# Gates of all dense tiles but one added into cleared DRAM by indirect DMAs, and 65 of 256 candidate sums

## Chip, cores and metric

The kernel runs on one core of a Trainium2 chip. The metric is the device time of one execution in microseconds (us). Names of engines: PE is TensorE, DVE is VectorE, ACT is ScalarE, POOL is GpSimd, SP is SyncE, which here only issues DMAs. ACT and POOL issue DMAs too.

## What is computed

Two layers of a trunk over 256 context tokens and 512 latent tokens, 1024 features wide: a mixer (attention and a short convolution in layer 0, an mLSTM in layer 1), and after each a feed-forward block that selects experts (PEER). The change lies in the PEER blocks:

```python
q = (xb @ w_q).reshape(PEER_BLOCK, PEER_HEADS, 2, PEER_DHALF)      # 8 heads, 2 halves
s = jnp.einsum('thpd,hpkd->thpk', q, subkeys)                      # 128 scores per half
s1, i1 = lax.top_k(s[:, :, 0], PEER_TOPK)                          # 16 of 128
s2, i2 = lax.top_k(s[:, :, 1], PEER_TOPK)
cand = (s1[..., :, None] + s2[..., None, :]).reshape(..., 256)     # 16 x 16 sums
cidx = (i1[..., :, None] * 128 + i2[..., None, :]).reshape(..., 256)
top, pos = lax.top_k(cand, PEER_TOPK)                              # 16 of 256
idx = jnp.take_along_axis(cidx, pos, axis=-1)
g = jax.nn.softmax(top, axis=-1)
act = jax.nn.gelu(jnp.einsum('td,thkd->thk', xb, u[idx]), approximate=False)
return jnp.einsum('thk,thkd->td', g * act, v[idx])
```

So each token takes 8 x 16 of 16,384 experts.

## The kernel before

**Tiles.** 128 tokens are one tile; the block of layer 0 has six tiles, that of layer 1 has four. Of these, `NG` = 2 and 1 are gathered: for each of the 128 (head, k) columns of a tile one indirect DMA on POOL's queue fetches 128 rows of `u` (512 KB, tile `urows`, `dot`, L899), and DVE multiplies them with the tokens (L905). The other tiles, four and three, are dense: all 16,384 rows of `u` and `v` pass PE.

**Two stages of a block.** `peer_u` runs over 128 chunks of 128 experts. In chunk c, SP loads `uf`, ACT and DVE split it into `uh` and `ul`, PE multiplies the dense tokens with it (24 matmuls, `proj`, L674), and ACT writes the Gelu to DRAM (`gad`). Chunks 0 to 16 also hold the 16 projection steps: `w_q` and `subk` are loaded and split (`q_load`, the low parts on POOL), PE projects all tokens, and DVE finds the 16 best of 128 scores for each tile (`topk16`). `peer_v0` and `peer_v1` then run over 128 chunks of `v`: they load `gad` and the gates `gd`, multiply them on DVE and feed PE.

**Gates.** A dense tile needs its gates as a matrix over tokens and experts. `stage2` finds the 16 best of 256 sums (`cands`, `decode`, `soft`). Then DVE writes one-hot matrices for eight tokens at a time (`prep`, L834 to L837, four instructions), PE multiplies them (`gbuild`, L851: 256 small matmuls for a tile), ACT copies the product into `stg`, and ACT's queue stores it into `gd`, 512 KB at a time.

**What sets the order.** `peer_u` shares out the work of routing, gates and gathered dots over the chunks: each item has a cost, each chunk has a budget (`slack`), and the queue with the largest share left goes next. `issue_after` ties an item to the split of the next chunk. A scheduler then fixes the sequence of each engine. Each engine runs its own sequence strictly in order. A DMA issued by SP or ACT counts on one of eight semaphores, which are taken in turn, and one issued by POOL on one of eight others; before a semaphore is used again, the DMA that used it last must have landed.

Of the kernel before, what the change touches and what calls it, by code (L numbers as in the profile page):

```python
# [10 lines left out]
F32 = mybir.dt.float32  # L11
# [10 lines left out]
P = 128  # L22
# [40 lines left out]
NG = (2, 1)  # L63
SEGS = ((0, NCTX), (NCTX, NLAT))
# [7 lines left out]
def kernel(ctx: ExitStack, tc: tile.TileContext, a: dict, out: bass.AP, dbg=None, stop=None):  # L72
# [13 lines left out]
    tok = [a["tok"][t * P:(t + 1) * P, :] for t in range(NT)]  # L86

# [125 lines left out]
    def mixer0(pk_open):  # L213
        with ExitStack() as st:
            rst = ExitStack()
            mcp = mkpool(st, "m0mc")
            mch = mcp.tile([P, 4, T], F32R, name="mch")
            mcl = mcp.tile([P, 4, T], F32R, name="mcl")
# [10 lines left out]
            with ExitStack() as s1:  # L229
# [225 lines left out]
            with ExitStack() as st2:  # L455
# [193 lines left out]
    def peer_u(layer, tiles):  # L649
# [4 lines left out]
        gd = dram.tile([TD // 32, P, P, 32], F32, name=f"gd{layer}")  # L654
# [3 lines left out]
        with ExitStack() as s1:  # L658
# [9 lines left out]
            def proj(ps, wh, wl, blks):  # L668
                for k in range(KD):
                    for x, q in ((wh, 0), (wh, 1), (wl, 0)):  # L670
# [9 lines left out]
                      allow_small_or_imprecise_dtypes=True)  # L680
            urow = [up.tile([P, P], U32, name=f"urow{j}", bufs=1) for j in range(ng)]
            gact = [up.tile([P, P], F32, name=f"gact{j}", bufs=1) for j in range(ng)]
# [5 lines left out]
            def q_load(hp):  # L688
# [4 lines left out]
                split(wh, wl, w, eng_lo=vec if hp < 2 else pool)  # L693
# [4 lines left out]
                split(skh, skl, sk, eng_lo=pool)  # L698
# [42 lines left out]
            side, pend, stores = [], [], []  # L741

            def store():
                b, stg, j = stores.pop(0)
                js = slice(j, j + P // GS)
                nc.scalar.dma_start(gd[b][:, js], stg[:, js])
# [5 lines left out]
            def stage2(t):  # L752
                d = {}

                def alloc():
                    d["top"] = up.tile([P, PH, TOPK], F32, name="top", bufs=3)
                    d["pos"] = up.tile([P, PH, TOPK], U32, name="pos", bufs=3)
                    d["if"] = up.tile([P, 16, TOPK], F16, name="if16", bufs=3)
                    d["id"] = [up.tile([P, PH, TOPK], F32, name=f"id{q}", bufs=3) for q in range(2)]

                def cands(h0):
                    def f():
                        vv = v16[t].rearrange("p (h q) k -> p h q k", q=2)
                        c = up.tile([P, 2, TOPK, TOPK], F32, name="cand", bufs=1)
                        hs = slice(h0, h0 + 2)
                        vec.tensor_tensor(c, vv[:, hs, 0, :, None].to_broadcast([P, 2, TOPK, TOPK]),
                                          vv[:, hs, 1, None, :].to_broadcast([P, 2, TOPK, TOPK]), op=ALU.add)
                        for h in range(2):
                            w_ = up.tile([P, 256], F32, name="candw", bufs=1)
                            topk16(d["top"][:, h0 + h, :], d["pos"][:, h0 + h, :],  # L770
                                   c[:, h].rearrange("p x y -> p (x y)"), w_)
                    return f

                def decode(h0):
                    def f():
                        iv = d["if"].rearrange("p (h q) k -> p h q k", q=2)
                        hs = slice(h0, h0 + 2)
                        qs = slice(2 * h0, 2 * h0 + 4)
                        vec.tensor_copy(d["if"][:, qs], i16[t][:, qs])
                        for q in range(2):  # L780
                            pi = up.tile([P, 2, TOPK], U32, name="pi")
                            if q == 0:
# [855 lines left out]
```

## Time and profile before

| | before |
|---|---|
| median of 3 runs | 4072.93 us (4070.59 to 4076.04) |
| profiled execution | 4070.86 us, of which the span of its instructions is 4069.1 us |
| `peer_u`, layer 0: projection steps | 475 to 785 us |
| `peer_u`, layer 0: the other 111 chunks | 785 to 1604 us |
| `peer_v0` | 1632 to 2310 us |
| `peer_u`, layer 1: the other 111 chunks | 2942 to 3504 us |
| `peer_v1` | 3549 to 4045 us |

Each stage has its own limit, so the shares of the whole span say little; the stages are read apart. A row with an arrow in brackets gives the idle time of an engine just before an instruction and what ended it. The chain of waits is followed back from the last instruction and shows, at each time, the work that nothing else would have hidden.

### The profile page before, as it was taken

What the parts mean: (1) busy time and instruction counts of PE and PEld (TensorE: products, weight loads), DVE (VectorE), ACT (ScalarE), POOL (GpSimd) and SP (SyncE); (2) the same over time, 40 slices, a digit from 0 to 9 for tenths busy, and PEclk for the clock granted to TensorE, in tenths of its full rate; (3) what the DMA queues carried; (4) which work ended last, traced back from release to release, by engine and by line L of the source; (5) the groups of instructions that cost most, each with busy time, mean ns of one, the idle gap of its engine ahead of it and who ended that gap; (6) DMA issues with size and microseconds to landing.
All of it is one profiled execution on the core that took longest, in us unless ns stands there. A gap on an engine that the chain in (4) does not pass through costs nothing. (4 is left out here: it accounts for less than half of the span.)

```text
span 4069.1 us, 53545 instructions
## 1 busy us (share of the span) xinstructions
PE 3779.4 (93%) x19201; PEld 3221.3 (79%) x19201; DVE 3287.3 (81%) x6594; ACT 1463.4 (36%) x2384; POOL 1394.4 (34%) x1010
## 2 busy tenths in 40 slices
PE   6988989999999897999999989888999999899998
PEld 5766777877777675788888789867899999788887
DVE  7776698998999897888888864458898987588887
ACT  4354422233232333322232355542234344333333
POOL 2521225303423244666666412215302222132221
PEclk9999989999999998999999999988999999999999
DMA  7301446548979799999999721046448779799995
GB/s 245 100 3 52 172 141 240 177 167 301 342 261 356 274 368 363 387 390 390 387 391 389 283 84 46 18 172 220 164 159 319 266 268 331 286 385 363 356 356 216
DMA packets 409099, 1036.47 MB, mean 255 GB/s; under 512 B 33024, under 2 KB 167680, under 8 KB 408832
## 3 DMA queue, kind: packets, MB, share of 16 engines
q1 hardware_dynamic: 259360, 498.68, 35.3%
q0 software_dynamic: 114336, 416.34, 27.9%
q10 hardware_dynamic: 35136, 118.05, 7.5%
q8 instruction: 150, 2.46, 0.2%
q14 instruction: 117, 0.96, 0.1%
HBM read 906.05 MB, written 126.88 MB: 254 GB/s over the span
## 5 line engine op out<-in xcount | busy, mean ns | idle before, releaser
L899 POOL DMA_INDIRECT urows<-in_u_rows,urow x384 | 487.5, 1270 | 1124.1 <-DVE urows L905 639.4
L1048 POOL DMA_INDIRECT vrows<-in_v_t,vrow x384 | 594.2, 1547 | 592.5 <-DVE accg L1056 340.1
L674 PE MATMUL aps<-pnh,uh 128*128 128x512 f32 (+1 forms) x2048 | 770.0, 376 | 22.0 <-ACT ga L991 18.4
L674 PE MATMUL aps<-pnh,ul 128*128 128x512 f32 (+1 forms) x2048 | 763.6, 373 | 26.3 <-DVE ul L109 26.0
L674 PE MATMUL aps<-pnl,uh 128*128 128x512 f32 (+1 forms) x2048 | 759.6, 371 | 0.0
L106 ACT CAST uh<-uf 128x1024 fp32r<-128x1024 f32 x256 | 269.2, 1051 | 839.2 <-PE aps L674 815.9
L905 DVE SCALAR_TENSOR_TENSOR urows<-urows,px 128x1024 f32<-128x1024 f32 x384 | 468.7, 1231 | 66.1 <-DMA urows<-in_u_rows,urow 65.4
L106 ACT CAST vh<-vf 128x1024 fp32r<-128x1024 f32 x256 | 269.3, 1053 | 594.5 <-DMA vf<-in_v_t 279.9
L674 PEld LDWEIGHTS aps<-pnh,ul 128*128 128x128 f32 x2048 | 389.8, 190 | 78.7 <-DVE ul L109 34.2
L674 PEld LDWEIGHTS aps<-pnh,uh 128*128 128x128 f32 x2048 | 391.5, 191 | 72.0 <-ACT ga L991 25.4
L109 DVE TENSOR_TENSOR vl<-vf,vh 128x1024 fp32r<-128x1024 f32 x256 | 312.6, 1221 | 166.0 <-ACT vh L106 155.9
L674 PEld LDWEIGHTS aps<-pnl,uh 128*128 128x128 f32 x2048 | 390.5, 191 | 43.2
L109 DVE TENSOR_TENSOR ul<-uf,uh 128x1024 fp32r<-128x1024 f32 x256 | 320.2, 1251 | 79.5 <-ACT uh L106 70.3
L1079 PE MATMUL acc<-vh,vwh 128*128 128x512 f32 x1024 | 317.7, 392 | 23.9 <-ACT vwh L106 23.8
L1079 PE MATMUL acc<-vh,vwl 128*128 128x512 f32 x1024 | 317.3, 391 | 1.3 <-DVE vwl L109 1.1
L1079 PE MATMUL acc<-vl,vwh 128*128 128x512 f32 x1024 | 317.5, 391 | 0.0
L1056 DVE SCALAR_TENSOR_TENSOR vacc<-vrows,gw,vacc 128x1024 f32<-128x1024 f32 x254 | 313.8, 1277 | 0.0
L851 PE MATMUL gps<-p,p 128*128 128x128 f16 x1792 | 243.9, 296 | 14.1 <-DVE p L837 14.1
L1144 PE MATMUL acc<-vh,vwh 128*128 128x512 f32 x768 | 239.3, 393 | 15.2 <-ACT vwh L106 12.1
L1079 PEld LDWEIGHTS acc<-vh,vwh 128*128 128x128 f32 x1024 | 192.8, 189 | 66.2 <-ACT vwh L106 26.4
L851 PEld LDWEIGHTS <-p 128*128 128x128 f16 x1792 | 189.1, 118 | 62.7 <-issue 38.6
L1144 PE MATMUL acc<-vl,vwh 128*128 128x512 f32 x768 | 238.2, 392 | 0.0
(430 smaller groups left out, 7540.8 us busy)
## 6 DMA issues: line engine op xcount, KB each, us to landing
uf<-in_u_t SPq DMA_DIRECT2D x256, 512.0 KB
vf<-in_v_t SPq DMA_DIRECT2D x256, 512.0 KB
gd<-stg ACTq DMA_DIRECT2D x112, 512.0 KB
wmt<-in_w_modT SPq DMA_DIRECT2D x90, 512.0 KB
gad<-ga ACTq DMA_DIRECT2D x64, 512.0 KB
gaf<-gad SPq DMA_DIRECT2D x64, 512.0 KB
gf<-gd SPq DMA_DIRECT2D x32, 1024.0 KB
gad<-ga ACTq DMA_DIRECT2D x64, 384.0 KB
```

Of the source, the lines that this page charges most:

```text
L106: act.copy(hi, src)
L109: return el.tensor_tensor(lo, src, hi.bitcast(F32), op=ALU.subtract)
L674: pe.matmul(ps[:, o:o + w], x[:, k, :], blk[q][:, k, :w], start=(k == 0 and x is wh and q == 0), stop=(k == KD - 1 and x is wl))
L851: pe.matmul(gp[:, i * P:(i + 1) * P], p1[:, g, :, i], p2[q][:, g, :, i], start=q == 0, stop=q == 1)
L899: nc.gpsimd.indirect_dma_start(out=r, out_offset=None, in_=a["u_rows"], in_offset=bass.IndirectOffsetOnAxis(ap=urow[j][:, k:k + 1], axis=0))
L905: vec.scalar_tensor_tensor(r, r, 1.0, PK["x"][j], op0=ALU.mult, op1=ALU.mult, accum_out=gact[j][:, k:k + 1])
L1048: nc.gpsimd.indirect_dma_start(out=r, out_offset=None, in_=a["v_t"].rearrange("l c k d -> (l c k) d"), in_offset=bass.IndirectOffsetOnAxis ...
L1056: vec.scalar_tensor_tensor(acc, r, gw[:, k:k + 1], acc, op0=ALU.mult, op1=ALU.add)
L1079: pe.matmul(acc[i][hf], x[:, ts_], y[:, hf * 512:(hf + 1) * 512], start=(c == 0 and first), stop=(c == 127 and end))
L1144: pe.matmul(acc[i][hf], x[:, ts_], y[:, hf * 512:(hf + 1) * 512], start=(c == 0 and first), stop=(c == 127 and last))
```

## The change

`NOH` = 1 dense tile keeps the one-hot products. For the others (three in layer 0, two in layer 1) five DRAM tiles of 4 x 128 x 128 x 32 floats, 8.4 MB each, are first set to zero by `clear`, a DMA on ACT's queue. When half of a tile's heads are routed, `spots` (DVE) computes for each token and (head, k) the place of its gate. `scatter` then issues an indirect DMA on POOL's queue for one (head, k): it adds 128 floats, one of each token, to their places. A tile has 128 such DMAs, so there are 384 in layer 0 and 256 in layer 1. Two of them on the same tile may hit the same place, and the later one waits until the earlier has landed; `scatter` goes round the tiles that are ready. A quota spreads them over the chunks up to `SC_END` = 122.

Candidate sums: only pairs whose ranks can be among the best 16 are formed, 65 of 256, for two or four heads at a time. `q_load` splits on DVE instead of POOL. In a projection step `topk16` comes last. The shares are now four queues with a chunk to begin and one to end each (`goal`), and the next item is that of the queue which lags most, in us.

```diff
+NOH = 1
+SC_END = 122
...
+    gds = [[dram.tile([4, P, P, 32], F32, name=f"gd{v}_{t}") for t in range(n - NG[v])]
+           for v, n in enumerate((NT, NLAT // P))]
+
+    def clear(v, t, zero):
+        nc.scalar.dma_start(gds[v][t].rearrange("b p j t -> (b p j t)").rearrange("(p x t) -> p x t", p=P, t=P),
+                            zero[:, None, :].to_broadcast([P, P, P]))
...
                 for j in range(3):
                     conv(j)
+                    if NOH + j < len(gds[0]):
+                        clear(0, NOH + j, zero)
...
+                    if h < len(gds[1]) - NOH:
+                        clear(1, NOH + h, zero)
...
-                split(wh, wl, w, eng_lo=vec if hp < 2 else pool)
+                split(wh, wl, w)
...
+                        c = up.tile([P, H, 65], F32, name="cand", bufs=1)
+                        for o, r0, rn, m in ((0, 0, 1, 16), (16, 1, 2, 8), (32, 3, 4, 4), (48, 7, 8, 2), (64, 15, 1, 1)):
+                            vec.tensor_tensor(c[:, :, o:o + rn * m].rearrange("p h (r m) -> p h r m", m=m),
...
+                def spots(h0):
+                    def f():
+                        ks, (i0, i1) = ids(h0)
+                        rf = up.tile([P, 4 * TOPK], F32, name="rowf", bufs=1)
+                        vec.tensor_scalar(rf, i0, float(P * 32), spos[:, 0:1], op0=ALU.mult, op1=ALU.add)
+                        vec.scalar_tensor_tensor(srow[t][:, ks], i1, 32.0, rf, op0=ALU.mult, op1=ALU.add)
+                        ready[t] += range(ks.start, ks.stop)
+                    return f
...
+                    return [(cands(h0), 1.6 * H, need), (decode(h0), 0.7 + 1.4 * H, need), (soft(h0), 1.0, need)] + \
+                        ([(last, 0.5, need)] if last else [])
...
+            queues = [route, one, dots, bgq]
+            goal = [(4, 66), (17, 114), (6, 125), (17, 124)]
...
+            def lag(q, c):
+                c0, c1 = goal[q]
+                want = min(max((reach[c] - reach[c0]) / (reach[c1] - reach[c0]), 0.0), 1.0)
+                return want * whole[q] - (whole[q] - left[q])
...
+                nc.gpsimd.indirect_dma_start(
+                    out=gd[t - ng].rearrange("b p j (t o) -> (b p j t) o", o=1),
+                    out_offset=bass.IndirectOffsetOnAxis(ap=srow[t][:, k:k + 1], axis=0),
+                    in_=g[:, k:k + 1], in_offset=None, compute_op=ALU.add)
...
+                quota = (scat - sent["n"]) if c == 127 else -(-(scat - sent["n"]) // max(SC_END - c, 1))
...
-                    q = max(ok, key=lambda q: left[q] / whole[q])
+                    q = max(ok, key=lambda q: lag(q, c))
...
+                    if quota > 0 and w > 1.0 and scatter():
+                        quota -= 1
+                while quota > 0 and scatter():
+                    quota -= 1
...
-            nc.sync.dma_start(st["gf"], gd[:, :, c:c + 4, :].rearrange("b p j t -> p b j t"))
+            for t, x in enumerate(gd):
+                nc.sync.dma_start(st["gf"][:, 4 * t:4 * t + 4], x[:, :, c:c + 4, :].rearrange("b p j t -> p b j t"))
```

The sequence of the engines shows where the new DMAs stand. A row is a line of the kernel, an operation and its tiles (with buffer numbers), and the semaphores that it waits for.

POOL in the middle of `peer_u`, layer 0. Before, gathers alone:

```order
L899 DMA urows_9351<-in_u_rows,urow1_4266 128x1024 [waits DMASW1_49,DVE_49]
L899 DMA urows_9354<-in_u_rows,urow0_4265 128x1024 [waits DMASW2_49,DVE_49]
L899 DMA urows_9390<-in_u_rows,urow1_4266 128x1024 [waits DMASW3_49,DVE_49]
L899 DMA urows_9401<-in_u_rows,urow0_4265 128x1024 [waits DMASW4_49,DVE_49]
L899 DMA urows_9442<-in_u_rows,urow1_4266 128x1024 [waits DMASW5_49,DVE_49]
```

In the change (`gd0_1` to `gd0_3` are the three tiles that take the sums, `srow` the places):

```order
L944 DMA urows_8641<-in_u_rows,urow1_4297 128x1024 [waits DMASW3_49,DVE_49]
L1030 DMA gd0_1_79<-g3_4304,srow3_4298 2097152x1 [waits DMASW0_49]
L1030 DMA gd0_3_81<-g5_4306,srow5_4300 2097152x1 [waits DMASW1_49]
L1030 DMA gd0_2_80<-g4_4305,srow4_4299 2097152x1 [waits DMASW2_49]
L944 DMA urows_8680<-in_u_rows,urow0_4296 128x1024 [waits DMASW7_49,DVE_49]
L1030 DMA gd0_1_79<-g3_4304,srow3_4298 2097152x1 [waits DMASW4_49]
```

Three scatters now stand between two gathers, and each waits for the scatter on its own tile four places ahead of it.

POOL at the end of `peer_u`, layer 0. Before, the last gathers of `u` are followed by loads and gathers of `peer_v0`:

```order
L899 DMA urows_13932<-in_u_rows,urow0_4265 128x1024 [waits DMASW6_49,DVE_49]
L899 DMA urows_13935<-in_u_rows,urow1_4266 128x1024 [waits DMASW7_49,DVE_49]
L1085 DMA vht_19664<-hd0_0_60 128x1024 [waits DMASW0_49,PE_49]
L1085 DMA vht_19679<-hd0_1_61 128x1024 [waits DMASW1_49]
L1048 DMA vrows_14370<-in_v_t,vrow0_3506 128x1024 [waits DMASW2_49,Pool_49]
```

In the change:

```order
L944 DMA urows_13114<-in_u_rows,urow0_4296 128x1024 [waits DMASW6_49,DVE_49]
L1030 DMA gd0_3_81<-g5_4306,srow5_4300 2097152x1 [waits DMASW7_49,DVE_49]
L944 DMA urows_13120<-in_u_rows,urow1_4297 128x1024 [waits DMASW0_49,DVE_49]
L1030 DMA gd0_3_81<-g5_4306,srow5_4300 2097152x1 [waits DMASW7_49,DMASW1_49]
L1030 DMA gd0_3_81<-g5_4306,srow5_4300 2097152x1 [waits DMASW2_49,DMASW1_49]
L1169 DMA vht_18783<-hd0_0_60 128x1024 [waits DMASW3_49,PE_49]
L1030 DMA gd0_3_81<-g5_4306,srow5_4300 2097152x1 [waits DMASW4_49,DMASW2_49]
```

64 scatters on one tile stand here in a row, behind all gathers of the stage but one; each waits for the one before it.

SP at the start of the program. Before:

```order
L272 DMA xn2_164<-in_tok 128x1024 [waits DMAHW1_49]
L148 DMA wmt_168<-in_w_modT 128x1024 [waits DMAHW2_49]
L253 DMA wmp_175<-in_w_mod0 128x1024 [waits DMAHW3_49]
L272 DMA xn3_186<-in_tok 128x1024 [waits DMAHW4_49]
L272 DMA xn4_190<-in_tok 128x1024 [waits DMAHW5_49]
```

In the change, where ACT's third DMA is the first clear (`gd0_1`), which counts on DMAHW4:

```order
L282 DMA xn2_173<-in_tok 128x1024 [waits DMAHW2_49]
L156 DMA wmt_177<-in_w_modT 128x1024 [waits DMAHW3_49]
L263 DMA wmp_184<-in_w_mod0 128x1024 [waits DMAHW4_49]
L282 DMA xn3_195<-in_tok 128x1024 [waits DMAHW5_49]
L282 DMA xn4_199<-in_tok 128x1024 [waits DMAHW6_49]
```

The load of `wmp` now waits for the clear, and the loads behind it wait with it.

## Rows read from the trace of the kernel before

**Rows 1.** The page: each engine's busy time, share and instructions
```profile
PE 3779.4 (93%) x19201; PEld 3221.3 (79%) x19201; DVE 3287.3 (81%) x6594; ACT 1463.4 (36%) x2384; POOL 1394.4 (34%) x1010
```

**Rows 2.** Busy time by stage; the first row names the columns
```profile
core 0: us, PE busy (x) PEld busy (x) DVE busy (x) ACT busy (x) POOL busy (x), PEclk, DMA share, GB/s
475.00:785.00 310.00, 283.46 (x1463) 243.48 (x1464) 272.99 (x995) 76.24 (x117) 124.63 (x89) 0.93 0.60 202
785.00:1604.00 819.00, 764.67 (x3692) 602.17 (x3692) 753.46 (x1585) 255.20 (x362) 253.73 (x201) 0.98 0.81 295
...
2942.00:3504.00 562.00, 556.29 (x3383) 543.76 (x3382) 478.67 (x947) 218.56 (x325) 104.72 (x88) 0.99 0.73 259
```

**Rows 3.** Chain of waits, end of peer_u, layer 1: start, us, what
```profile
3479.23 1.90 PE gps L851 x16
3481.13 4.25 PE aps L674 x24
...
3504.64 2.64 DMA gd<-stg
3507.35 8.25 DMA gf<-gd
```

**Rows 4.** Groups on DVE, 475 to 1615 us: busy, mean ns, idle
```profile
L905 DVE SCALAR_TENSOR_TENSOR urows<-urows,px 128x1024 f32<-128x1024 f32 x256 | 309.4, 1220 | 58.4 <-DMA urows<-in_u_rows,urow 57.6 <-DVE p2e L835 0.4
...
L837 DVE TENSOR_TENSOR p<-p2e,idT 128x1024 f16<-128x1024 f16 x128 | 83.1, 682 | 0.0
...
L834 DVE TENSOR_TENSOR p<-iota,idT 128x1024 f16<-128x1024 f16 x64 | 43.7, 684 | 0.0
L835 DVE TENSOR_TENSOR p2e<-iota,idT 128x1024 f16<-128x1024 f16 x64 | 43.6, 680 | 0.0
...
L644 DVE FIND_INDEX8 i<-v,sc 128x8 uint32<-128x128 f32 x96 | 27.1, 282 | 0.0
...
L644 DVE FIND_INDEX8 pos<-top,cand 128x8 uint32<-128x256 f32 x48 | 20.0, 416 | 0.0
...
L109 DVE TENSOR_TENSOR wql<-wq,wqh 128x1024 fp32r<-128x1024 f32 x2 | 2.5, 1226 | 3.6 <-ACT wqh L106 3.6
```

**Rows 5.** Gathers of u: ns shortest/median/longest, first and last start
```profile
L899 POOL DMA_INDIRECT urows<-in_u_rows,urow x384: 932/1145/2304, 591.0 to 3468.0; - x192
```

**Rows 6.** Groups on POOL, 785 to 1604 us
```profile
L899 POOL DMA_INDIRECT urows<-in_u_rows,urow x198 | 251.8, 1272 | 579.6 <-DVE urows L905 303.9 <-DVE urow L870 146.5 <-DVE pi L785 106.1
```

**Rows 7.** POOL in time: layer 1's first gathers, one of layer 0
```profile
2792.78 0.99 POOL L899 DMA_INDIRECT urows<-in_u_rows,urow  x1 [3.84 <-DVE rowf L869]
2794.08 0.97 POOL L899 DMA_INDIRECT urows<-in_u_rows,urow  x1 [0.30 <-issue]
...
1019.57 0.94 POOL L899 DMA_INDIRECT urows<-in_u_rows,urow  x1 [3.89 <-DVE urows L905]
```

**Rows 8.** DVE in time: the dots that waited for those gathers
```profile
2797.27 1.23 DVE L905 SCALAR_TENSOR_TENSOR urows<-urows,px 128x1024 f32<-128x1024 f32 x1 [0.35 <-DMA urows<-in_u_rows,urow]
...
1026.61 1.22 DVE L905 SCALAR_TENSOR_TENSOR urows<-urows,px 128x1024 f32<-128x1024 f32 x1 [0.44 <-DMA urows<-in_u_rows,urow]
```

**Rows 9.** Busy time in the first 160 us, columns as in rows 2
```profile
0.00:10.00 10.00, 0.00 (x0) 0.00 (x0) 0.27 (x1) 3.41 (x3) 0.70 (x6) 1.00 0.77 244
10.00:20.00 10.00, 6.69 (x31) 6.66 (x32) 5.05 (x11) 5.24 (x9) 0.00 (x0) 1.00 1.02 410
20.00:30.00 10.00, 3.95 (x18) 3.81 (x18) 7.51 (x17) 4.61 (x9) 4.38 (x3) 1.00 1.02 394
30.00:160.00 130.00, 109.25 (x586) 95.03 (x587) 121.67 (x225) 50.55 (x118) 49.25 (x33) 0.95 0.57 173
```

**Rows 10.** DMA issues of SP at the start: start us, us, line
```profile
6.18 0.52 SPq L253 DMA_DIRECT2D wmp<-in_w_mod  x1
```

More of the change, by code (lines that the diff above doesn't have):

```diff
@@ L653, in peer_u @@
         TD = TT - ng * P
-        gd = dram.tile([TD // 32, P, P, 32], F32, name=f"gd{layer}")
+        gd = gds[layer]
         gad = dram.tile([64, P, 2, TD], F32, name=f"gad{layer}")
@@ L752, in stage2 @@
             def stage2(t):
[L753 to L759, printed above, removed]
+                H = 2 if t < ng else 4
+                keep = ng <= t < ng + NOH
@@ L761, in cands @@
+                d = {"id": up.tile([P, 2, PH, TOPK], F32, name="idk", bufs=NOH)} if keep else {}
                 def cands(h0):
                     def f():
[L763 to L771, printed above, removed]
+                        hs = slice(h0, h0 + H)
+                        top = d["top"] = up.tile([P, H, TOPK], F32, name="top")
+                        pos = d["pos"] = up.tile([P, H, TOPK], U32, name="pos")
+                        vv = v16[t].rearrange("p (h q) k -> p h q k", q=2)[:, hs]
@@ L772, in cands @@
+                        for h in range(H):
+                            w_ = up.tile([P, 65], F32, name="candw", bufs=1)
+                            topk16(top[:, h, :], pos[:, h, :], c[:, h, :], w_)
                     return f
@@ L945, in peer_u @@
                         if len(pend) > 3:
-                            side.append((pend.pop(0), 0.0))
-                        if nxt:
-                            side.append(nxt.pop(0))
-                side += nxt
-            side += [(f, 0.0) for f in pend] + [(flush, 0.0)]
-            queues = [early, [(f, w, 2 * PH) for f, w in side], [(f, 1.33 * (2 if layer == 0 and x < 24 else 1), 0) for x, f in enumerate(bg)]]
-            left = [sum(x[1] for x in q) for q in queues]
-            whole = [x + 1e-6 for x in left]
+                            one.append((pend.pop(0), 0.0, 0))
@@ new lines, in peer_u @@
+            one += [(f, 0.0, 0) for f in pend] + [(flush, 0.0, 0)]
+            total_dots = P * ng
+            dots = [(dot(x), 1.3, (x, 1)) for x in range(total_dots)] + [(st2[t][4], 0.3, (total_dots - 1, 1)) for t in range(ng)]
+            bgq = [(f, 1.33 * (2 if layer == 0 and x < 24 else 1), 0) for x, f in enumerate(bg)]
+            queues = [route, one, dots, bgq]
+            goal = [(4, 66), (17, 114), (6, 125), (17, 124)]
+            whole = [sum(x[1] for x in q) for q in queues]
+            left = list(whole)
@@ new lines, in lag, with can @@
+            def lag(q, c):
+                c0, c1 = goal[q]
+                want = min(max((reach[c] - reach[c0]) / (reach[c1] - reach[c0]), 0.0), 1.0)
+                return want * whole[q] - (whole[q] - left[q])
+            def can(q, c):
+                if not queues[q]:
+                    return False
+                need = queues[q][0][2]
+                return need[0] < at["rows"] if isinstance(need, tuple) else need <= c or c == 127
+            sent = {"n": 0, "t": 0}
+            scat = P * len(ready)
```

179 lines of the change are left out of this document (107 added, 72 removed).

## The prediction

> **What bounds the kernel now.** First the page: PE is busy 93% of the span, DVE 81%, POOL 34% [rows 1]. These are averages, so the table of stages comes next; the reader is to see which engine is full in each. In layer 0 from 785 us on, PE works 764.67 and DVE 753.46 of 819 us: both are nearly full. In layer 1 PE works 556.29 of 562 us and bounds alone. The projection steps of layer 0 have PE at 283 and DVE at 273 of 310 us, a mixture of both [rows 2]. POOL works 254 of 819 us in layer 0 and 105 of 562 in layer 1, so it has room, but each gather is followed by a dot on DVE, and the order has 2 to 3 gathers a chunk. The chain of waits shows what the seam costs at the end of layer 1: products of the gates (`gps`, 16 matmuls in 1.90 us) alternate with the projection (`aps`), then the last store of gates lands (2.64 us) and the first load of `gf` takes 8.25 us [rows 3]. `peer_v` waits for the whole gate matrix, so whatever finishes `gd` last delays it.
>
> **What the change takes away.** Three tiles in layer 0 and two in layer 1 lose their one-hot products. A tile has 32 groups of eight matmuls, and sixteen matmuls take 1.90 us [rows 3], so PE is freed of 96 x 0.95 = 91 us and 64 x 0.95 = 61 us. DVE loses 16 `prep` a tile, each of four instructions near 0.68 us [rows 4]: in layer 0, 48 x 2.73 = 131 us. A search through 256 sums takes 416 ns and one through 128 scores 282 ns, a slope of 1.05 ns an element [rows 4]; 65 sums save 191 x 1.05 = 0.20 us on each of five instructions of 48 heads, 48 us. Against this stand the low parts of `w_q` on DVE, 1.226 us each [rows 4], some 17 us. By busy time alone PE would then set a chunk: (764.67 - 91)/111 = 6.1 us in layer 0 in place of 7.4, and (556 - 61)/111 = 4.5 us in layer 1 in place of 5.06. The projection steps I leave as they are in layer 0: DVE's smaller sums and larger splits meet there, and PE's work is the same.
>
> **What it adds: prices.** A scatter is an indirect DMA on POOL; none is in the trace. Its price on POOL: gathers take 932 ns at the shortest, 1145 in the middle, and 1272 ns on the mean of this stage [rows 5, 6], and 0.30 us goes by between two [rows 7]. I take 1.05 + 0.30 = 1.35 us, between 1.24 and 1.57: a scatter writes as many addresses as a gather, one for each of 128 partitions. I see no reason for much less.
>
> The second price matters more. Two scatters on one tile must not overlap, and the order shows that the later one waits for the earlier's landing. The step from one to the next is then issue, flight and gap. The nearest rows: the gather that POOL began at 2792.78, when little else ran, let its dot start at 2797.27, 4.49 us later; a gather begun at 1019.57 under load let its dot start at 1026.61, 7.04 us later [rows 7, 8]. The dots wait for other things as well, so I read these as a light and a loaded size of a 512 KB gather. At 410 GB/s [rows 9] 512 KB occupy 1.28 us, so a scatter, with 512 bytes, would need 4.49 - 1.28 = 3.2 us with its issue; the landing of a store, 2.64 us [rows 3], says about the same. I take 3.4 us in an empty stretch and 4.0 us beside the loads of `u`. The ends are 1.24 us (nothing but issue and gap) and 4.5 us in the empty stretch, 7.0 us under load.
>
> [...]
>
> **Layer 0, chunk by chunk.** The gathers and scatters were counted in the order. In chunks 18 to 41, 59 scatters stand almost all on one tile, because only one has its places computed: 59 x 4.0 = 236 us, where PE asks 24 x 6.1 = 146; the 42 gathers fit between them. In chunks 42 to 96 three tiles take turns, so the landing is covered and POOL's rate decides: 118 gathers and 237 scatters, 355 x 1.35 = 479 us against PE's 336. In chunks 97 to 110, 24 scatters on one tile: 96 us. Chunks 111 to 127 have gathers alone: 17 x 6.1 = 104 us. Then the tail. The last `spots` of `route` is an item of 0.5 us, and the new rule takes the queue that lags most in us; with half a microsecond left that queue is nearly always passed over until chunk 126. So 64 scatters of one tile stand in a row at the end, each waiting for the one before, and `peer_v0` waits for them: 64 x 3.4 - 12 (what the last chunks cover) = 206 us. With 6 us for chunk 17 the sum is 1127 us in place of 819: **+308**. POOL is thus the engine that turns late: DVE's dots wait for gathers behind scatters, the split of the next chunk stands behind these dots on DVE, and PE waits for the split.
>
> **Layer 1.** Ten scatters on one tile among the projection steps, 40 us where 26 lie free: +14. In chunks 18 to 44, 33 serial steps, 132 us; in chunks 45 to 98 two tiles alternate, 51 pairs and 34 single ones, 85 steps of 4.0 = 340 us; chunks 99 to 127, 29 x 4.5 = 130; the tail, again 64 on one tile, 64 x 3.4 - 15 = 203. With 4.5 for chunk 17, 810 in place of 562: **+248**.
>
> **The start.** The clears stand at the very head of ACT's sequence, and the semaphore of the first is that for which SP's load of `wmp` waits; it was issued at 6.18 us before [rows 10]. The first 30 us move 10.5 MB, up to 410 GB/s, and the next 130 us 22.5 MB [rows 9]. Until `wmp`, 4.2 MB and the clear's 8.4 MB must land: 12.6/0.41 = 31 us, and SP stands some 27 us longer. All five clears, 42 MB, make 75 MB of the first 160 us' demand, 183 us at that rate, 23 over. The two overlap in part; **+45**, between 27 and 90.
>
> The seams and `peer_v` I cost at nothing: `gf` now comes in four or three DMAs of the same bytes, issued by SP beside loads that are four chunks early, and PE is full there; if that cover is gone, it is 3 x 0.5 us of issue [rows 10] for each of 32 loads, 48 us. The profiled execution was 4070.86 us, 2 below the median. The sum: 4071 + 308 + 14 + 248 + 45 = 4686, forecast **4685 us**.
>
> **Rivals.** (1) The scatters land quickly. With a step of 2.3 us, half a gather, and 1.24 on POOL, layer 0 is 6 + 146 + 440 + 85 + 104 + 135 = 916 (+97), layer 1 632 (+70), the start +27: 4265 us, and 4480 halfway to the forecast. For it: 512 bytes instead of 512 KB. Against it: no DMA in these rows took less than 2.6 us. (2) They land slowly: adding means reading the place first, then writing it, and 128 places lie apart. With 4.4 us in the tails and 5.0 under load it is 1274 (+455) and 991 (+429), q +24, start +45: 5025 us; with the upper ends everywhere 1524 and 1234, q +44, start +90, about 5580 us. (3) **Faster**: POOL hands a scatter over much faster than a gather. If it takes 0.5 us and 0.3 of gap, the middle of layer 0 is 118 x 1.24 + 237 x 0.80 = 336, just PE's own need, and all but the tails is hidden. Then the gains stand: -145 in layer 0, -61 in layer 1, +27 at the start, -27 that the last chunks cover of the tails, and 128 serial steps R: -206 + 128 R, faster below R = 1.61 us; at 1.24 us it gives 4024 us. Against it speak all 384 gathers, none under 0.93 us [rows 5], and the flight. (4) That the tail isn't at the end, so that the scheduler's order does not hold on the chip, has no room: each engine runs its sequence as it stands.
>
> One more row bears on POOL's price: the same gather took from 932 to 2304 ns [rows 5]. [...]
>
> **How the numbers follow.** Forecast 0.51 (4480 to 4880), quick landing 0.20, slow landing 0.20, faster 0.07; within 0.2%, which is about what a measurement of this kernel can tell from no change, 0.02. Slower is then 0.91. To hold eight in ten, the range takes in the forecast's case, most of the quick one and the middle of the slow one: 4280 to 5080 us.
>
> **What the profile after would show.** Scatters on POOL near 1.05 us each and 640 in number; 512 small products of the gates in place of 1792; searches of 65 sums near 0.22 us. At the end of each `peer_u` some 200 us in which PE is idle and POOL's scatters each wait for a DMA on the same tile, 3.4 us apart. In the middle of layer 0 DVE's dots waiting for `urows`, with POOL near full. At the start, SP waiting until about 33 us for `wmp`. What would make it wrong: a step far from 3.4 us (128 hang on it in the tails and 201 under load), an issue far from 1.05 us, or clears that are written slower than 410 GB/s.

## The result, and the profile after

The change makes the kernel slower: 5111.68 us (median; 5090.8 to 5120.94) against 4071.76 us, a ratio of 1.2549 (95% interval 1.2502 to 1.2595). The forecast was 4685 us, the range ended at 5080. The direction and the places are those of the prediction; the loss is 1020 us in the profiled execution (span 5089.0 against 4069.1 us) where 615 were worked out.

The page of the kernel after, engines first (answers to [rows 1]), then its new group and the clears among the DMA issues:

```profile
PE 3780.6 (74%) x17906; PEld 3205.2 (63%) x17906; DVE 3037.1 (60%) x6423; ACT 1418.7 (28%) x2273; POOL 2364.0 (46%) x1604
...
L1030 POOL DMA_INDIRECT gd<-g,srow x640 | 1083.4, 1693 | 728.8 <-DMA gd<-g,srow 499.1
...
gd<-zero ACTq DMA_DIRECT2D x5, 8192.0 KB, 39.9
```

PE no longer fills the span, and nothing else does either. POOL has 970 us more of work (its 640 scatters alone make 1083), and stands for another 499 us before a scatter until an earlier one has landed. DVE's dots stand for gathered rows, and PE's products for DVE's split of `u`. These are the two groups on the pages of before and after (busy time, mean ns, idle time before them and for whom):

```profile
L905 DVE SCALAR_TENSOR_TENSOR urows<-urows,px 128x1024 f32<-128x1024 f32 x384 | 468.7, 1231 | 66.1 <-DMA urows<-in_u_rows,urow 65.4
L674 PE MATMUL aps<-pnh,ul 128*128 128x512 f32 (+1 forms) x2048 | 763.6, 373 | 26.3 <-DVE ul L109 26.0
```

```profile
L950 DVE SCALAR_TENSOR_TENSOR urows<-urows,px 128x1024 f32<-128x1024 f32 x384 | 467.9, 1223 | 859.3 <-DMA urows<-in_u_rows,urow 858.9
L688 PE MATMUL aps<-pnh,ul 128*128 128x512 f32 (+1 forms) x2048 | 834.2, 407 | 487.5 <-DVE ul L117 487.4
```

The stages tell where this counts. Their limits are the starts of chunks 17, 42, 97, 111 and 127 in layer 0 and of 46, 100 and 127 in layer 1, read from DVE's splits of `u`, and the first matmul of `peer_v` (columns as in [rows 2]: stretch, length, busy time of PE, PEld, DVE, ACT and POOL, granted clock, DMA share, GB/s):

```profile
20.00:40.00 20.00, 0.00 (x0) 0.00 (x0) 0.00 (x0) 0.00 (x0) 0.00 (x0) 1.00 1.09 317
...
861.00:1085.00 224.00, 169.82 (x704) 134.49 (x703) 133.08 (x413) 55.30 (x72) 119.78 (x82) 0.88 0.61 172
1085.00:1756.00 671.00, 409.61 (x1398) 310.69 (x1398) 320.98 (x765) 111.81 (x145) 553.35 (x356) 0.77 0.67 168
1756.00:1912.00 156.00, 102.14 (x416) 79.23 (x417) 85.00 (x131) 27.05 (x38) 102.13 (x68) 0.80 0.80 243
1912.00:2040.00 128.00, 108.36 (x471) 85.34 (x470) 94.55 (x154) 33.29 (x45) 66.17 (x46) 0.92 0.95 352
2040.00:2282.00 242.00, 11.69 (x56) 8.98 (x56) 15.34 (x30) 5.75 (x11) 115.42 (x78) 0.53 0.27 55
...
3734.00:4185.00 451.00, 290.16 (x1423) 280.59 (x1422) 194.08 (x385) 97.65 (x136) 321.56 (x207) 0.80 0.63 159
...
4338.00:4550.00 212.00, 7.04 (x41) 6.72 (x39) 1.45 (x2) 1.18 (x4) 101.61 (x71) 0.53 0.19 24
```

In chunks 42 to 96 of layer 0 POOL works 553 of 671 us in 356 instructions. Of the 118 us left, 97 are gaps of some 0.3 us between one instruction and the next, and 14 are waits for landings (the two groups below). POOL is the bound there, with PE at 61%. In the two rows of 242 and 212 us PE and DVE do next to nothing: these are the tails. At 20 to 40 us no engine works and the DMA engines are full: the first clear. The same limits in both profiles give the account:

| stage | before, us | after, us | difference | predicted |
|---|---|---|---|---|
| start to the projection steps of layer 0 | 473 | 594 | +121 | +45 |
| projection steps, layers 0 and 1 | 295 and 217 | 267 and 204 | -41 | +14 |
| layer 0, chunk 17 to `peer_v0` | 864 | 1421 | +557 | +308 |
| layer 1, chunk 18 to the end | 1129 | 1510 | +381 | +248 |
| `peer_v0` and the mixer of layer 1 | 1091 | 1093 | +2 | 0 |

SP's queue at the start of the kernel after (start, duration, line) stands between two loads, and 34.7 us of it are a wait for the first clear, which lands at 41.6 us; [rows 10] had this `wmp` at 6.18 us:

```profile
6.47 0.45 SPq L156 DMA_DIRECT2D wmt<-in_w_modT  x1
41.64 0.33 SPq L263 DMA_DIRECT2D wmp<-in_w_mod  x1
```

POOL in the tail of layer 1, in order of time (start, duration, in brackets the idle time before it and what ended it):

```profile
4370.66 1.55 POOL L1030 DMA_INDIRECT gd<-g,srow  x1 [1.84 <-DMA gd<-g,srow]
4373.96 1.55 POOL L1030 DMA_INDIRECT gd<-g,srow  x1 [1.75 <-DMA gd<-g,srow]
4377.24 1.55 POOL L1030 DMA_INDIRECT gd<-g,srow  x1 [1.73 <-DMA gd<-g,srow]
```

A step is 3.3 us (3.4 were predicted), but its make-up is not the one that was assumed: 1.55 us on POOL instead of 1.05. In the middle of layer 0 it is 1.72 us on the mean (POOL's groups in chunks 42 to 96; count, busy, mean ns, idle before):

```profile
L1030 POOL DMA_INDIRECT gd<-g,srow x238 | 408.6, 1717 | 82.0 <-issue 67.6 <-DMA gd<-g,srow 14.4
L944 POOL DMA_INDIRECT urows<-in_u_rows,urow x118 | 145.7, 1234 | 36.0 <-issue 29.3 <-DVE urows L950 2.1 <-DVE pt L819 0.6
```

The gathers beside them take 1.23 us, near the 1.27 of [rows 6], so it is the scatter alone that is dearer than a gather.

### The profile page after: what moved, and what is told of

Read it like the earlier page. It is cut to its first block, busy times and chain, and to the rows that moved or that the text cites. A ratio compares the mean times of both kernels' runs of the same rounds, so it can differ in the third digit from the quotient of the medians.

```text
span 5089.0 us, 51493 instructions
## 1 busy us (share of the span) xinstructions
PE 3780.6 (74%) x17906; PEld 3205.2 (63%) x17906; DVE 3037.1 (60%) x6423; ACT 1418.7 (28%) x2273; POOL 2364.0 (46%) x1604
## 5 line engine op out<-in xcount | busy, mean ns | idle before, releaser
L1030 POOL DMA_INDIRECT gd<-g,srow x640 | 1083.4, 1693 | 728.8 <-DMA gd<-g,srow 499.1
L688 PE MATMUL aps<-pnh,ul 128*128 128x512 f32 (+1 forms) x2048 | 834.2, 407 | 487.5 <-DVE ul L117 487.4
L950 DVE SCALAR_TENSOR_TENSOR urows<-urows,px 128x1024 f32<-128x1024 f32 x384 | 467.9, 1223 | 859.3 <-DMA urows<-in_u_rows,urow 858.9
L688 PE MATMUL aps<-pnh,uh 128*128 128x512 f32 (+1 forms) x2048 | 821.0, 401 | 29.5 <-ACT ga L1069 25.9
L688 PE MATMUL aps<-pnl,uh 128*128 128x512 f32 (+1 forms) x2048 | 812.3, 397 | 0.0
L688 PEld LDWEIGHTS aps<-pnh,ul 128*128 128x128 f32 x2048 | 432.2, 211 | 577.8 <-DVE ul L117 524.8
L688 PEld LDWEIGHTS aps<-pnh,uh 128*128 128x128 f32 x2048 | 433.9, 212 | 84.6 <-ACT ga L1069 29.0
L688 PEld LDWEIGHTS aps<-pnl,uh 128*128 128x128 f32 x2048 | 429.6, 210 | 54.9
L1121 DVE TENSOR_TENSOR gaf<-gaf,gf 128x512 f32<-128x512 f32 (+1 forms) x256 | 158.0, 617 | 444.0 <-DMA gf<-gd 438.1
L114 ACT CAST vwh<-gaf 128x512 fp32r<-128x512 f32 (+1 forms) x256 | 144.5, 564 | 684.5 <-DVE gaf L1121 644.1
L1163 PE MATMUL acc<-vl,vwh 128*128 128x512 f32 x1024 | 316.6, 391 | 0.0
```

Of the source, the lines that this page charges most:

```text
L114: act.copy(hi, src)
L688: pe.matmul(ps[:, o:o + w], x[:, k, :], blk[q][:, k, :w], start=(k == 0 and x is wh and q == 0), stop=(k == KD - 1 and x is wl))
L950: vec.scalar_tensor_tensor(r, r, 1.0, PK["x"][j], op0=ALU.mult, op1=ALU.mult, accum_out=gact[j][:, k:k + 1])
L1030: nc.gpsimd.indirect_dma_start(out=gd[t - ng].rearrange("b p j (t o) -> (b p j t) o", o=1), out_offset=bass.IndirectOffsetOnAxis(ap=srow[t ...
L1121: vec.tensor_tensor(w3, w3, st["gf"][:, :, c % 4, :], op=ALU.mult)
L1163: pe.matmul(acc[i][hf], x[:, ts_], y[:, hf * 512:(hf + 1) * 512], start=(c == 0 and first), stop=(c == 127 and end))
```

## Experiments

The theory after these rows has three parts: POOL's time for a scatter bounds the middle of both layers, the landing of scatters on one tile makes the tails, and the clears make the late start. The rivals stand in the expectations. All ratios are to the kernel before.

**Without scatters.** `scatter` returns at once:

```diff
+                return False
                 t = min(ts_, key=lambda x: ((x - sent["t"] - 1) % n))
```

> All 640 scatters are left out (the gates of three tiles of layer 0 and two of layer 1 stay zero); clears, places, sums and the rest as in the change. Theory A (POOL's scatters and their tails make the whole loss of peer_u): layer 0 after chunk 17 falls to PE's floor, some 690 us, layer 1 to some 510, with the start still 121 us late: about 3970 us. Theory B (the chunks have another floor, such as the loads and the dots, near what they had before): layer 0 820, layer 1 560, about 4150 us.

Measured: 3964.69 us, ratio 0.9733 (0.9716 to 0.9749); theory A's time within 6 us. So the 640 scatters cost 1147 us, 1.8 us each, though the start is still late by the clears. From chunk 17 to `peer_v` it gains 110 us on the kernel before in layer 0 and 78 in layer 1, where theory A had 129 and 52, so its sum agrees better than its parts. Stages from chunk 42 of layer 0 on, and the middle of layer 1, show the floors that the prediction had put at 6.1 and 4.5 us a chunk:

```profile
1022.00:1375.00 353.00, 330.80 (x1420) 261.99 (x1418) 316.15 (x771) 114.66 (x148) 159.87 (x120) 0.97 0.89 320
1375.00:1471.00 96.00, 93.13 (x430) 74.89 (x429) 83.11 (x131) 27.43 (x39) 47.58 (x34) 0.98 1.01 390
1471.00:1596.00 125.00, 106.39 (x466) 84.22 (x465) 98.71 (x165) 33.59 (x46) 64.94 (x42) 0.93 0.98 377
...
3027.00:3268.00 241.00, 241.00 (x1412) 239.89 (x1411) 197.31 (x400) 96.70 (x133) 76.67 (x60) 1.00 0.86 300
```

In the middle PE is near full again, at 6.4 and 4.4 us a chunk. Chunks 111 to 126 of layer 0 stay at 125 us, as before the change (127): there the DMA engines are full (0.98, and 0.96 before), and PE freed of its products has nothing to gain. The prediction had counted 104. That floor depends on what the shares put into these chunks: the kernel without any scattered tile, below, moves 41 MB there instead of 47 and takes 117 us.

**Scatters that write instead of adding:**

```diff
-                    in_=g[:, k:k + 1], in_offset=None, compute_op=ALU.add)
+                    in_=g[:, k:k + 1], in_offset=None)
```

> The scatters write instead of adding (where a token takes an expert twice, one of the two gates is lost); waits and order stay. Theory A (POOL's 1.58 us for a scatter is the price of writing 128 addresses of 4 bytes each): unchanged, 1.55 to 1.6 us and 3.3 us a step in the tail, 5090 to 5130 us. Theory B (the add makes it dear, in POOL's issue by 0.6 us against a gather's 0.95 or in the landing by a read ahead of the write): 0.95 us on POOL or a step of 2.5 us, layer 0's middle 150 us less, about 4750 us.

Measured: 4739.59 us, ratio 1.1639 (1.1619 to 1.1658); theory B's time, 372 us less than the change. Its tail of layer 0 on POOL:

```profile
2000.18 0.97 POOL L1030 DMA_INDIRECT gd<-g,srow  x1 [1.43 <-DMA gd<-g,srow]
2002.59 0.97 POOL L1030 DMA_INDIRECT gd<-g,srow  x1 [1.44 <-DMA gd<-g,srow]
2004.99 0.97 POOL L1030 DMA_INDIRECT gd<-g,srow  x1 [1.43 <-DMA gd<-g,srow]
```

Writing 128 places takes POOL 0.97 us, as a gather does; the add makes it 1.55. From the start of the instruction to its landing it is 2.1 us where the add has 3.0 (the trace's medians in the two tails), and the step is 2.41 us in place of 3.3. So the add costs 0.58 us of POOL's time and about 0.3 us of flight. Chunks 42 to 96 of layer 0 take 555 us instead of 671, with POOL at work for 414 of them and standing for landings for 40. This is the part that the rows of before could not show, since no DMA there adds.

**Every scatter on another tile than the one before it:**

```diff
-                    out=gd[t - ng].rearrange("b p j (t o) -> (b p j t) o", o=1),
+                    out=gd[NOH + sent["n"] % len(ready)].rearrange("b p j (t o) -> (b p j t) o", o=1),
```

> Each scatter goes to the next of the cleared tiles in turn (three in layer 0, two in layer 1) whatever token tile its gates are of, so gates land in the wrong matrix; number, order and price of the scatters are those of the change, but two in a row are never on one tile. Theory A (where scatters of one tile stand in a row the landing decides, 3.28 us a step, and elsewhere POOL's issue, 1.6 + 0.3): the tails fall to 64 x 1.9 = 120 us each, 2 x 88 less; chunks 18 to 41 of layer 0 lose some 30 us, the middle of layer 0 nothing, that of layer 1 some 80; about 4810 us. Theory B (landings are in series for a reason other than the tile, such as POOL's queue): unchanged, 5090 to 5130 us. With both tails and middle at POOL's issue, what is left over the kernel before is POOL's issue and the start.

Measured: 4812.83 us, ratio 1.1827 (1.1807 to 1.1846); theory A within 3 us. The tails fall from 242 to 145 us and from 212 to 123 us. POOL in the first of them:

```profile
2061.11 1.55 POOL L1030 DMA_INDIRECT gd<-g,srow  x1 [0.30 <-issue]
2062.97 1.55 POOL L1030 DMA_INDIRECT gd<-g,srow  x1 [0.30 <-issue]
2064.83 1.55 POOL L1030 DMA_INDIRECT gd<-g,srow  x1 [0.31 <-issue]
```

The same instruction with the same 1.55 us, now every 1.86 us: the wait was for the tile, and nothing else holds a scatter there. The split in parts missed in three places. Chunks 18 to 41 of layer 0 did not shorten (207 us against 208): as soon as the waits go, more scatters come into that stretch (66 against 46), and POOL is nearly full. Chunks 42 to 96 of layer 0, which were to lose nothing, took 634 us instead of 671, with 16 scatters fewer in them. And chunks 43 to 97 of layer 1 lost 24 us instead of some 80 (423 against 447).

**The last items of `route` first:**

```diff
-                    q = max(ok, key=lambda q: lag(q, c))
+                    q = 0 if 0 in ok and left[0] < 2.0 else max(ok, key=lambda q: lag(q, c))
```

> One line of the change: the last items of route (under 2 us left) go first, so the last 64 places of a tile are computed near chunk 66 and no run of 64 scatters is left at the end of peer_u. Theory A (each tail is 64 serial steps of 3.3 us that nothing covers; POOL has room for them from chunk 97 on): the 242 and 212 us between the last chunk and peer_v fall to near 50 us each, the middle chunks grow by some 30 us, in all 280 to 330 us less than the change, about 4800 us. Theory B (POOL is the bound of all of peer_u, so scatters that leave the tail lengthen the chunks by as much): 60 to 130 us less, about 5010 us.

Measured: 4905.26 us, ratio 1.2044 (1.2024 to 1.2064): 206 us less, between the two theories. The tails go almost as A says, to 72 and 65 us, but part of them comes back. These are chunks 111 to 126 of layer 0 and its tail, to be laid beside the rows of 128 and 242 us above:

```profile
1911.00:2098.00 187.00, 123.66 (x497) 95.24 (x495) 97.92 (x154) 33.38 (x48) 120.27 (x82) 0.83 0.77 247
2098.00:2170.00 72.00, 6.93 (x22) 5.22 (x22) 13.49 (x25) 2.76 (x6) 37.38 (x28) 0.56 0.56 176
```

The last chunks take 59 us more, and in layer 1 chunks 98 to 126 take 250 instead of 170 us. The gathers there now stand behind scatters of one tile that wait for each other: in the 187 us POOL stands for 47 before 40 scatters until an earlier one has landed.

**The clears later,** with zeros that are made from the last convolution:

```diff
-            vec.memset(zero, 0.0)
...
-                    if NOH + j < len(gds[0]):
-                        clear(0, NOH + j, zero)
...
+                vec.tensor_scalar(zero, mcl[:, 2, T - P:T], 0.0, None, op0=ALU.mult)
...
-                    if h < len(gds[1]) - NOH:
-                        clear(1, NOH + h, zero)
+                    if h + NOH < len(gds[0]):
+                        clear(0, NOH + h, zero)
+                    if 0 <= h - 3 < len(gds[1]) - NOH:
+                        clear(1, NOH + h - 3, zero)
```

> The five clears are made to wait for the last convolution (the zeros are made from its result) and are issued in the attention of layer 0, where DMA is idle; all else as in the change. Theory A (at the start the clears hold SP's loads and fill the DMA engines): the projection steps begin near 475 us as before the change, 110 to 120 us earlier, about 4990 us. Theory B (a clear blocks its semaphore and the loads behind it wherever it stands): half of it comes back in the attention, 50 us less, about 5060 us. The landing of a clear tells its own rate: 20 us if 8.4 MB move at the 410 GB/s of the loads, near 40 us if its packets of 512 bytes are slow by themselves.

Measured: 5045.28 us, ratio 1.2397 (1.2377 to 1.2418): 66 us less, nearer to theory B, but for another reason. The projection steps begin at 554 us, 40 us earlier than in the change. ACT's queue shows what holds them:

```profile
193.63 24.69 ACTq L93 DMA_DIRECT2D gd<-zero  x1
...
222.23 25.57 ACTq L93 DMA_DIRECT2D gd<-zero  x1
247.97 28.75 ACTq L93 DMA_DIRECT2D gd<-zero  x1
```

The first clear took 0.59 us to issue; each of the others holds ACT for 25 to 29 us, until about 3 us before the clear ahead of it lands. In the change, where they stand further apart, three took 0.5 to 0.6 us to issue and the last two 15.5 us each. And a clear is slow by itself: a clear lands after 30.7 us at best, 273 GB/s, and the stretch from 190 to 300 us moves 287 GB/s with the DMA engines full (1.02), where the loads at the start of the kernel before had 410 [rows 9].

**The same clears issued by SP:**

```diff
-        nc.scalar.dma_start(gds[v][t].rearrange("b p j t -> (b p j t)").rearrange("(p x t) -> p x t", p=P, t=P),
+        nc.sync.dma_start(gds[v][t].rearrange("b p j t -> (b p j t)").rearrange("(p x t) -> p x t", p=P, t=P),
```

> As the run with the late clears, but SP issues them. There a clear held ACT for some 26 us at its issue, four times, and all stood at 190 to 305 us. Theory A (what remained of the late start, 79 us, is ACT standing at the issue): SP has little to issue in the attention, so the projection steps begin near 480 us, 70 us under the run with ACT's clears, about 4975 us. Theory B (what remained is the DMA engines being full for 110 us, at 287 GB/s, with the loads of w0 and the later ones in between): 5020 to 5050 us.

Measured: 4979.76 us, ratio 1.2229 (1.2210 to 1.2247); theory A's time within 5 us. The projection steps begin at 495 us (480 were said), 22 us later than before the change, though SP is held for up to 28.9 us at a clear. From 190 to 300 us DMA is as full with SP as with ACT, but the other engines work (the run with ACT's clears, then this one):

```profile
190.00:300.00 110.00, 38.10 (x191) 32.72 (x190) 15.37 (x29) 13.49 (x25) 15.52 (x10) 0.69 1.02 287
```

```profile
190.00:300.00 110.00, 92.02 (x498) 75.00 (x496) 68.15 (x149) 58.12 (x122) 34.22 (x21) 0.95 1.02 285
```

So of the 121 us that the start lost, 40 came back by the later place and 59 by the other engine, which has less to do behind a clear; 22 remain.

**Both repairs:** the edit of `route`, and the clears late and by SP.

> Both repairs in one: the last items of route first (206 us by itself) and the clears issued late by SP (132 us by itself); all five tiles are still scattered. Theory A (the two losses lie in different stages and add up): 5112 - 206 - 132 = 4774 us, and what is left over the kernel before, some 700 us, is POOL in the middle of both layers. Theory B (they overlap): 4820 us or more.

Measured: 4810.79 us, ratio 1.1816 (1.1790 to 1.1842). 301 of the 338 us add up; the other 37 I did not follow. With all repairs of order the change is still 740 us behind the kernel before; by the run without scatters, which is under the kernel before even with the late start, what is left lies in the scatters.

**Fewer tiles scattered.** With `NOH = 2` and `NOH = 3` (and both repairs), and with `NOH = 4`, which leaves scatters and clears out. The edit for the last:

```diff
-NOH = 1
+NOH = 4
...
-            one = [x for t in range(ng, ng + NOH) for p in range(PH // 4) for x in st2[t][0](4 * p)]
+            one = [x for t in range(ng, min(n, ng + NOH)) for p in range(PH // 4) for x in st2[t][0](4 * p)]
```

> Two tiles of layer 0 and one of layer 1 are scattered (NOH = 2), 256 and 128 scatters; SP issues the three clears in the attention, and the last items of route go first. Theory A (POOL's issue decides in layer 0: 256 x 1.95 + 232 x 1.55 = 860 us after chunk 17 against 819 before the change; in layer 1, 128 x 1.95 + 128 x 1.55 = 450 us hide): layer 0 some 40 us longer than before, layer 1 some 30 us shorter, about 4060 us. Theory B (the serial landings decide in both layers, as each tile's 128 steps need 4 to 5 us): 4150 to 4250 us.

> One tile of layer 0 alone is scattered (NOH = 3), 128 scatters; its one clear is issued by SP in the attention of layer 0, and the last items of route go first. Theory A (POOL's time decides: 128 scatters of 1.9 us and 232 gathers of 1.55 us are 600 of 819 us, so they hide): PE is freed of 30 us and DVE of 44 in layer 0, about 3960 us, 20 to 40 under the same kernel with one-hot products for all. Theory B (128 serial steps of 4 to 5 us each hold the gathers behind them, 59 of them already in chunks 18 to 41 cost 48 us in the change): 40 to 80 us over that kernel, about 4060 us.

> All dense tiles keep the one-hot products (NOH = 4): no scatters, no clears, no places; the 65 sums, DVE's splits of w_q, the order of a projection step and the new shares stay. Theory A (the rest of the change is worth little: 48 us less on DVE in layer 0, which was nearly full beside PE, and some 40 us in the projection steps of both layers, as in the change): 60 to 100 us under the kernel before, about 3990 us. Theory B (layer 0 is bound by PE, 765 of 819 us, so DVE's gain goes nowhere): 0 to 30 us, about 4055 us.

Measured: 4525.39 us, ratio 1.1107 (1.1090 to 1.1124), with two tiles and one; 4218.39 us, ratio 1.0359 (1.0343 to 1.0375), with one; 4006.31 us, ratio 0.9838 (0.9824 to 0.9851), with none. The last, theory A's, is faster than both kernels, 1.6% under the one before: from the projection steps to `peer_v` it takes 1110 us in layer 0 and 775 in layer 1, against 1159 and 794 before. My expectations for the first two were far too low: neither theory came near 4525, and one tile alone costs 212 us over the kernel with none. Its POOL was to work 600 of 819 us and hide, so it is not POOL's total that decides. In chunks 42 to 96 of layer 0 DVE's dots (L950; idle before them, and for whom) read so, with one tile scattered and then with none:

```profile
L950 DVE SCALAR_TENSOR_TENSOR urows<-urows,px 128x1024 f32<-128x1024 f32 x111 | 135.0, 1222 | 109.4 <-DMA urows<-in_u_rows,urow 109.3
```

```profile
L950 DVE SCALAR_TENSOR_TENSOR urows<-urows,px 128x1024 f32<-128x1024 f32 x109 | 132.4, 1218 | 3.3 <-DMA urows<-in_u_rows,urow 3.3
```

DVE waits 109 us for gathered rows instead of 3. The gathers stand behind scatters on POOL's queue, and a wait of that queue is a wait of DVE and then of PE (859 and 487 us in the groups of the change above).

**How much of that is the landing?** One tile scattered as above, but in turn into its own matrix and two spare ones:

```diff
+    junk = [dram.tile([4, P, P, 32], F32, name=f"junk{q}") for q in range(2)]
...
-                    out=gd[t - ng].rearrange("b p j (t o) -> (b p j t) o", o=1),
+                    out=(gd[t - ng], *junk)[sent["n"] % 3].rearrange("b p j (t o) -> (b p j t) o", o=1),
```

> One tile of layer 0 scattered as in the run with NOH = 3 (4218 us, with one-hot products for all 4006), but the 128 scatters go in turn to the tile's own matrix and to two spare ones that nobody reads, so two thirds of the gates are lost and no scatter waits for one before it that has just been issued; two more clears by SP. Theory A (the 212 us come from POOL standing at a landing, 207 us by the profile, with the gathers behind it): 4000 to 4060 us; what is left over 4006 is POOL's issue and the run at the end, 64 steps no longer in series. Theory B (a scatter's issue, 1.9 us between two gathers, by itself starves DVE's dots): 4130 us or more.

Measured: 4137.96 us, ratio 1.0162 (1.0145 to 1.0179), near theory B. Of the 212 us, 80 are the landings (some 90, as the two additional clears start the projection steps 11 us later); 120 remain with scarcely a wait. By stages the tail falls from 125 to 57 us, as long as with none, and what remains lies mostly in chunks 42 to 96 (435 us against 384 with none) and 111 to 126 (173 against 117). POOL in chunks 42 to 96 there:

```profile
L948 POOL DMA_INDIRECT urows<-in_u_rows,urow x111 | 146.9, 1323 | 176.0 <-DVE urows L954 141.5 <-issue 13.1 <-DVE g L842 7.3
L1034 POOL DMA_INDIRECT junk<-g,srow x36 | 61.4, 1705 | 12.0 <-issue 10.4 <-DMA junk<-g,srow 1.3 <-DMA gd<-g,srow 0.3
```

POOL is idle for 176 us of 435 before gathers, and yet DVE's dots wait 73 us for rows. The scatters come in clumps: none between 1080 and 1430 us, and several between two gathers elsewhere, since the places of half a tile are computed at one time (the reason is read from the code). The wait goes with them: 69 of the 73 us lie between 936 and 1100 us, where POOL works 131 of 164 us and its gaps of 0.3 us make 25 more; from 1100 to 1371 us, with gathers alone, the dots wait 4 us. So where scatters stand, POOL is full, whatever its share of the stage. Whether an even spread of one tile's scatters would hide them wasn't tried.

**The low parts of `w_q` on POOL again,** with `NOH = 4`:

```diff
-                split(wh, wl, w)
+                split(wh, wl, w, eng_lo=vec if hp < 2 else pool)
...
-                split(skh, skl, sk)
+                split(skh, skl, sk, eng_lo=pool)
```

> As the kernel with one-hot products for all dense tiles, but the low parts of w_q and subk are split on POOL again, as before the change. Theory A (DVE is nearly full in the projection steps, 264 of 295 us before, so the 17 us that the change put on it are felt): 5 to 15 us less than 4006 in both layers together. Theory B (the larger split waits for POOL, 2.4 us instead of 1.23, and PE waits for it): 5 to 15 us more. If neither, the place of the split is worth nothing.

Measured: 4012.11 us, ratio 0.9860 (0.9844 to 0.9877), the same as 0.9838 within the intervals: where the low parts are split makes no difference that these runs can tell. Neither theory is borne out.

## Why the prediction was right and wrong

- **Right: the bound and the tails.** POOL turned late, with DVE waiting for gathers behind scatters and PE for DVE. 512 products of the gates are left and a search of 65 sums takes 0.22 us, as said. The two runs of 64 scatters were read from the order, and their step of 3.4 us from the landing of the gathers in [rows 7, 8] and of a store in [rows 3]: measured 3.3 us, 242 and 212 us in all, and the scatters on other tiles showed that the tile's landing makes it. The size of the step is in part luck: it is 1.55 us of issue and 1.75 of flight and gap, where 1.05 and 2.35 were assumed. A plain scatter steps every 2.41 us, which is what the quick rival took (2.3); so the gathers' landing is not a good measure of a scatter's, and the add made up the difference.
- **Wrong: the price of a scatter on POOL.** This is the step that failed first. "A scatter writes as many addresses as a gather" gave 1.05 us, with 1.57 for issue and gap as the upper end. That holds for a plain scatter (0.97 us in an empty stretch). One that adds takes 1.55 us in an empty stretch and 1.69 on the mean; with the gap 2.0 us, above the upper end. The middle of layer 0, 355 x 1.35 = 479 us in the sum, became 671; the plain scatter gave 555 there. So the add accounts for 116 of the 192 us missing, and the other 76 are gathers and scatters at 1.15 to 1.19 us beside other work, not 1.05, and waits for landings. The slow rival priced the add as a read and then a write, which no run here shows apart, and put its price into the flight, where the add costs 0.3 us, and not into the issue, where it costs 0.58. That its 5025 us lies near the measured time is chance: it has a step of 4.4 us in the tails, and an issue as cheap as a gather's.
- **Wrong: the gains of the last chunks.** Chunks 97 to 126 were to cost 96 + 104 us in layer 0 and 130 in layer 1; they took 156 + 128 and 153. In chunks 111 to 126 of layer 0 the DMA engines are full before the change (0.96) and after it (0.95), so what PE is freed of there is no gain. The DMA share was in [rows 2] only as the mean of the stage, 0.81. In chunks 97 to 110 33 scatters ran where 24 were counted, and POOL was never free: 103 us of work, 39 of waiting for landings, the rest gaps. In the last chunks of layer 1, counted without scatters, 14 ran and DVE's dots waited 34 us; without any scatters these chunks take the 134 us that PE asks. Against these losses, chunks 18 to 41 of layer 0 took 208 us where 236 were counted, with 46 scatters in them instead of 59.
- **Wrong: the middle of layer 1.** 85 serial steps of 4.0 us were counted, 340 us, as if the gathers lay inside them; it took 451 us, and POOL was hardly ever free: 322 us of work, 49 of gaps and 78 of waiting for landings. The group in chunks 46 to 99 of the kernel after:

```profile
L1030 POOL DMA_INDIRECT gd<-g,srow x150 | 254.4, 1696 | 110.7 <-DMA gd<-g,srow 78.0 <-issue 32.8
```

- **Half right: the start.** The order showed SP behind the first clear, and it stood until 41.64 us (33 were said). But the clears were priced at the loads' 410 GB/s; a clear moves at 273 at best, and the stretches that clears fill move 285 to 317. Nor was it counted that the fourth and fifth held ACT for 15.5 us each. The start lost 121 us, above the 90 of the upper end.
- **Wrong, the other way: the projection steps.** They were left as they are in layer 0 and put 14 us worse in layer 1; they gained 28 and 13 us. With `NOH` = 4 they take 285 and 211 us, a gain of 10 and 6, and the place of the low parts did not matter. How the rest divides between the smaller sums, the order of a step and the work that falls into these chunks is open.
- **The range** fell short by 32 us because the unknown issue was bounded by gathers alone. With 2.0 us a scatter the middles come to 118 x 1.55 + 237 x 2.0 = 657 us and 59 x 1.5 + 136 x 2.0 = 361 us at least, 178 and 21 more, which would have put the forecast near 4885. The rest of the gap to 5112 is in the terms above: gathers beside serial steps, waits for landings in the middles, and the clears.

## To carry to other kernels

A DMA that the queue has not carried yet has two unknown prices, the time on the issuing engine and the flight (here, in an empty stretch, 1.55 us and 3.0 us from the start to the landing for a scatter that adds, 0.97 and 2.1 us for one that writes); each needs its own row, and where only another kind of DMA has one, the upper end must lie well above it. A queue that carries gathers is to be priced as a path of its own, stretch by stretch: with one tile's scatters spread over three matrices, POOL stood idle before gathers for 176 of 435 us, and yet DVE's dots waited 69 us in the 164 us that the scatters fill. And a large fill is to be priced by the engine that issues it as well as by its bytes: the same five clears in the attention cost 59 us less of the start from SP than from ACT.

## What the runs showed of the hardware

- Indirect DMAs on POOL of 128 places of four bytes, in the tails: writing took 0.97 us of issue and landed 2.1 us after its start; adding took 1.55 and 3.0 us.
- A fill of 8.4 MB from a row of 512 bytes a partition landed after 30.7 us at best (273 GB/s), while loads of 512 KB reached 410 GB/s. With one clear and next to nothing beside it (`NOH` = 3, 202 to 222 us) the DMA engines were full (1.01 to 1.02) at 286 to 290 GB/s. A clear issued while another was under way held its engine, ACT or SP, until 2 to 3 us before that one landed: 25 to 29 us right behind another, 15.5 us for the last two of the change, 1.4 us where the one ahead was 3 us from landing (SP, both repairs); with none under way 0.5 to 0.6 us.
- PE's granted clock was 0.53 of full speed in the tails, where PE works 12 of 242 us and 7 of 212, and 0.77 in the middle of layer 0, where it works 410 of 671 us; before the change it was 0.98 over the stage [rows 2]. From 20 to 40 us, where PE does nothing, the column has 1.00.
- POOL's time for the same adding scatter was 1.55 us in the tails, where DVE hardly works, and 1.72 us on the mean in the middle of layer 0. Within that middle the trace parts the scatters by what DVE did in their first 1.5 us: 76 beside no work of DVE took 1.57 us on the mean, 55 beside a dot (L950) alone 1.56, and the other 106 took 1.90. So the extra time goes with some of DVE's instructions, and not with the load of the stage. Of the 106, the 17 that ran beside a cast or a tensor_scalar took 1.79 us, and the other 89 took 1.92. Which instructions do it is open, and no run here took DVE's work away by itself.
